# Hybrid mLSTM and latent-attention block on one core: nine changes to the order of splits, loads and turns beside an almost always busy TensorE

## The chip, the cores and the metric

One Trainium2 chip, one core of it. The metric is the device time of one execution in microseconds (us), as the median of several runs. A difference of 0.2% is 5.7 us here.

## The reference

One trunk layer of an encoder on 2048 tokens of width 1024, in f32:

```python
xn = rms_norm(h, ln_mix_g)
proj = xn @ w_in                           # 1024 -> 2512 columns
y_a = mlstm_group(q, k, v, o, gates, ...)  # 4 heads x 128, chunks of 128 tokens, both directions
y_b = mla_group(c_q, c_kv, k_rope, ...)    # latent attention, 4 heads, softmax over 2048 keys
h = h + concat([y_a, y_b]) @ w_out
h = h + (silu(gate) * val) @ w_down        # gate, val = dwconv3(rms_norm(h) @ w_up), width 2816
gate = sigmoid(rms_norm(h, ple_norm_g) @ w_ple_gate)
h = h + gate * rms_norm(p @ w_ple_proj, ple_post_g)
out = rms_norm(h, final_g)
```

## The kernel before

Every f32 product is made of three matmuls in a rounded f32 format: each operand is **split** into a high part (a cast on ScalarE, L121, or L129 with a factor) and a low part (source minus high part on VectorE, L124 or L130). Products of the big projections are made in **pairs** of output blocks by a seven-product scheme, whose operands are named A11, A12, A22, S1 to S4 (weights) and B11, B21, B22, T1 to T4 (activations); each pair runs a fixed sequence of products into the banks fx, fy, fz (L541 in the mLSTM projections, L1700 in output projection, MLP and gate). Between the products stand numbered calls `side(1)` to `side(7)`, which put other work into TensorE's order: transposes, splits, loads.

The stages, in order of time:

1. **in_proj**: 16 token tiles. For each, `rest` (product `bk<-wsr,xh`), `turn_rest` of the tile before (transposes `rtp`, L283), `vals` (product `bk<-wsp,xh`). POOL makes each tile's norm factor into a column of `rcol` (L142, L144). `norm_row` (L298) transposes 8 of these columns at once into a row, which is stored in `r_d` and read back as `rrow`. Beside it the activations' operands are made (`xsr`) and stored in `xo_d`.
2. **pairs** (twelve pairs): operands that don't stay resident are loaded from `xo_d` through four buffers `opr` and split in place; T3, T4 and B22 of the first half come through this queue during the first pair. `gates` is a generator whose steps (its yields) are run at every second side call; it makes the mLSTM gate factors and puts small matmuls (`fs<-ms`, L944) in between.
3. **queries**: for eight blocks c of 256 tokens, `latent` makes the no-rope queries (`qo`, L809), `rope` and `turn` the roped ones (`qro`, `qso`), stored in `q_d`. `attend_begin` starts attention inside this loop: it loads the first queries (`q_t`, L1145), splits them (`q_s`), and makes the first tile's scores (`bk<-kv,q_s`, L1163 to L1167).
4. **attend**: for every head and query tile the scores, maximum, exponential, transposes (`tb<-ident,pe`, L1227) and values (`ppv<-pt,kv`). The mLSTM runs beside it as a generator: at each of the order's pauses `pump` adds SIDE/(tiles x pauses) to an account, and one step of the generator runs when the account reaches one. SIDE is meant as the number of its steps. `pause(n)` yields n times. A chunk of the mLSTM loads `kn_d` into `kk` (w12), scales it (L999, in `state`), and at its end multiplies its sum `hh` by a factor, pauses, transposes it (`mb<-ident,hy`, L1130) and stores it.
5. **stream** (pairs -8 to 75): output projection (i < 0), up, down and gate. `up_prep` makes a pair's weight operands by `prep_a` and `prep_b`; `Out.turn` (L1998) transposes normalised tiles of the output projection, `Gate.turn` (L2122) tiles `ha` of the MLP's result into `gwr`.

TensorE's order is written out by hand (a manual schedule); what the other engines do follows the order in which the code issues it, with some instructions pinned to it (`keep_in_program_order`). All DMAs are issued from SyncE (SP). Buffers are fixed places: tags w, t, u, x with a number, each reused by many tiles, so that a place's new tile waits for the last reader of the one before.

## Time and profile before

| | us |
|---|---|
| median of 3 runs (lowest, highest) | 2856.83 (2855.85, 2857.14) |
| profiled execution | 2859.16 |
| its span | 2857.4 |
| outside the span | 1.76 |
| TensorE (PE) busy | 2816.5 (99%) |
| weight loads (PEld) busy | 2363.5 (83%) |
| VectorE (DVE) busy | 2131.6 (75%) |
| ScalarE (ACT) busy | 1581.6 (55%) |
| GpSimd (POOL) busy | 211.1 (7%) |
| DMA: mean rate, moved | 193 GB/s, 552.73 MB |

The profiled execution is 2.33 us above the median. A row of the timeline gives start, duration, engine, line, operation and `out<-in` by the program's names, how many equal instructions it stands for, and in brackets how long the engine was idle before it and what released it. A row of the table by windows gives each engine's busy time in a stretch, the granted TensorE clock (1.00 is full speed) and the busy share of the DMA engines.

### The profile page before, as it was taken

What the parts mean: (1) busy time and instruction counts of PE and PEld (TensorE: products, weight loads), DVE (VectorE), ACT (ScalarE), POOL (GpSimd) and SP (SyncE); (2) the same over time, 40 slices, a digit from 0 to 9 for tenths busy, and PEclk for the clock granted to TensorE, in tenths of its full rate; (3) what the DMA queues carried; (4) which work ended last, traced back from release to release, by engine and by line L of the source; (5) the groups of instructions that cost most, each with busy time, mean ns of one, the idle gap of its engine ahead of it and who ended that gap; (6) DMA issues with size and microseconds to landing.
All of it is one profiled execution on the core that took longest, in us unless ns stands there. A gap on an engine that the chain in (4) does not pass through costs nothing.

```text
span 2857.4 us, 39996 instructions
## 1 busy us (share of the span) xinstructions
PE 2816.5 (99%) x13932; PEld 2363.5 (83%) x13932; DVE 2131.6 (75%) x3702; ACT 1581.6 (55%) x3072; POOL 211.1 (7%) x331
## 2 busy tenths in 40 slices
PE   8999998999999999999999999999999999999998
PEld 7888887888888888888888888888888888888787
DVE  4877766777887777877778787777778767676787
ACT  6346765555566566655655556655556333254655
POOL 2100000000000000044200000000000000011012
PEclk9999999999999999999999999999999999999999
DMA  8883758554443333578735544667776757575864
GB/s 281 288 250 113 214 161 243 159 172 128 130 131 116 99 112 107 156 244 276 254 134 199 176 169 162 199 199 229 238 237 209 236 192 237 171 266 200 287 202 163
DMA packets 444531, 552.73 MB, mean 193 GB/s; under 512 B 34564, under 2 KB 296744, under 8 KB 444328
## 3 DMA queue, kind: packets, MB, share of 16 engines
q1 hardware_dynamic: 444328, 550.16, 60.1%
q8 instruction: 110, 1.80, 0.3%
q14 instruction: 93, 0.76, 0.1%
HBM read 357.45 MB, written 192.61 MB: 193 GB/s over the span
## 4 chain that ended last, share of the span: by engine, by line
PE 84%; DVE 4%; DMA 3%; ACT 2%; issue 1%; POOL 0%; SPq 0%; POOLq 0%; ACTq 0%; DVEq 0%
PE fy L1700 22%; PE fz L1700 15%; PE fx L1700 14%; PE ppv L1239 4%; PE tb L1227 3%; PE fy L541 3%; PE fz L541 2%; PE ppv L1240 2%; PE bk L1163 2%; PE bk L1165 2%; PE bk L1166 2%; PE bk L1164 2%; PE bk L1167 2%; PE fx L541 2%; PE fs L134 2%; PE mb L1101 1%
## 5 line engine op out<-in xcount | busy, mean ns | idle before, releaser
L1700 PE MATMUL fz<-op,fw 128*128 128x512 f32 x1968 | 479.3, 392 | 3.8 <-ACT fw L121 3.8
L1700 PE MATMUL fx<-op,fw 128*128 128x512 f32 x1968 | 476.0, 390 | 0.0
L1700 PE MATMUL fy<-op,fw 128*128 128x512 f32 x1968 | 475.2, 390 | 0.0
L1700 PEld LDWEIGHTS fz<-op,fw 128*128 128x128 f32 x1968 | 368.5, 188 | 81.9 <-ACT fw L121 5.0
L1700 PEld LDWEIGHTS fy<-op,fw 128*128 128x128 f32 x1968 | 368.7, 188 | 77.0 <-DVE fh L1685 0.5
L1700 PEld LDWEIGHTS fx<-op,fw 128*128 128x128 f32 x1968 | 368.4, 188 | 75.9
L121 ACT CAST pt<-tb 128x512 fp32r<-128x512 f32 x256 | 147.5, 586 | 187.9 <-PE tb L1227 187.0
L1700 PE MATMUL fy<-op,fwd 128*128 128x512 f32 (+1 forms) x984 | 238.1, 390 | 0.0
L1168 DVE TENSOR_REDUCE mx<-bk 128x1 f32<-128x512 f32 x256 | 175.4, 686 | 67.2 <-PE bk L1167 64.8
L1700 PEld LDWEIGHTS fy<-op,fwd 128*128 128x128 f32 x984 | 182.9, 188 | 37.7 <-DVE uv L1685 0.4
L124 DVE TENSOR_TENSOR pt<-tb,pt 128x512 fp32r<-128x512 f32 x256 | 173.5, 686 | 33.4 <-ACT pt L121 32.7
L1239 PE MATMUL ppv<-pt,kv 128*128 128x512 f32 x512 | 188.6, 407 | 1.0 <-DVE pt L124 1.0
L1185 ACT ACTIVATE pe<-bk,nm 128x512 f32<-128x512 f32 x256 | 174.7, 698 | 21.2 <-DVE nm L1179 21.1
L124 DVE TENSOR_TENSOR fw<-fwr,fw 128x1024 fp32r<-128x1024 f32 x124 | 150.9, 1221 | 34.0 <-ACT fw L121 32.7
L121 ACT CAST op<-opr 128x512 fp32r<-128x512 f32 x205 | 120.7, 620 | 81.2 <-DMA opr<-xo_d 16.6
L124 DVE TENSOR_TENSOR op<-opr,op 128x512 fp32r<-128x512 f32 x205 | 134.6, 690 | 25.7 <-ACT op L121 25.5
L1227 PE MATMUL tb<-ident,pe 128*128 128x128 f32 x1024 | 150.5, 273 | 1.5 <-DVE pt L124 1.3
L121 ACT CAST fw<-fwr 128x1024 fp32r<-128x1024 f32 x124 | 129.7, 1051 | 37.3 <-DVE fwr L1674 21.3
L1240 PE MATMUL ppv<-pt,kv 128*128 128x256 f32 x512 | 144.2, 282 | 0.0
L1227 PEld LDWEIGHTS tb<-ident,pe 128*128 128x128 f32 x1024 | 122.2, 141 | 20.4 <-DVE pt L124 4.1
L121 ACT CAST fw<-hraw 128x1024 fp32r<-128x1024 f32 (+1 forms) x72 | 70.2, 980 | 115.8 <-PE fx L1700 58.8
L1748 DVE SCALAR_TENSOR_TENSOR fgv<-uv,fcw,fgv 128x1024 f32<-128x1024 f32 x88 | 112.8, 1282 | 16.0 <-ACT fgv L1746 9.5
(407 smaller groups left out, 5210.1 us busy)
## 6 DMA issues: line engine op xcount, KB each, us to landing
fwr<-in_w_up SPq DMA_DIRECT2D x66, 512.0 KB
fh<-h_d SPq DMA_DIRECT2D x48, 512.0 KB
h_d<-fh SPq DMA_DIRECT2D x48, 512.0 KB
s_d<-fwr SPq DMA_DIRECT2D x44, 512.0 KB
fws<-s_d SPq DMA_DIRECT2D x44, 512.0 KB
rw<-row_d SPq DMA_DIRECT2D x32, 512.0 KB
tw_d<-tsum SPq DMA_DIRECT2D x60, 256.0 KB
opr<-tw_d SPq DMA_DIRECT2D x60, 256.0 KB
```

Source lines behind the costliest of these rows:

```text
L121: nc.scalar.copy(hi, src)
L124: (sub or nc.vector).tensor_tensor(lo, src, _f(hi), op=ALU.subtract)
L134: mm = lambda *a, **k: self.nc.tensor.matmul(*a, **k, skip_group_check=more)
L541: nc.tensor.matmul(out, a[:, k * P:(k + 1) * P], parts[lo], start=first, stop=lo == 1 and k == 3, skip_group_check=more)
L1163: mm(ps, ql, kh[:, ks], start=True, stop=False)
L1168: nc.vector.tensor_reduce(s.mx[:, kb:kb + 1], ps, axis=AX.X, op=ALU.max)
L1185: nc.scalar.activation(s.pe[:, kb % 2], s.banks[kb], AF.Exp, bias=s.nm, accum_out=s.rs[:, kb:kb + 1])
L1227: nc.tensor.transpose(t[:, j, :], s.p[kb][:, j * P:(j + 1) * P], self.ident)
L1239: mm(w.ps, vh[:, ks], pts[kb][:, j], start=kt == 0, stop=False, skip_group_check=True)
L1240: mm(w.ps[:, 0], vl[:, ks], pts[kb][:, j, 0], start=False, stop=kt == NT - 1, skip_group_check=True)
L1700: nc.tensor.matmul(out, a[:, k * P:(k + 1) * P], parts[lo][:, cols], start=first, stop=lo == 1 and k == last, skip_group_check=more)
L1748: nc.vector.scalar_tensor_tensor(t, u[:, tap:tap + 2 * SB], self.taps[:, tap, ct:ct + 1], t, op0=ALU.mult, op1=ALU.add)
```

## The change

Nine places, in order of time:

- **A** in_proj: `norm_row` of tiles 3 and 5 moves from ahead of the tile's first product to behind `turn_rest`.
- **B** T3 of the first half is loaded by four DMAs into places w12 and w13 at the start of the pairs, and split from there; the queue `opr` carries T4 and B22 only.
- **C** gates: one more yield ahead of the matmul `fs<-ms`.
- **D** queries: `attend_begin` is called one block earlier (c = 3). It loads there, splits at c = 4, and makes the scores at c = 5 as before. The queries' split lies in the second half of their own tile, not in w2 or u2. `split_c(7)` comes one block earlier, and the next scores stand behind all of block 7's products.
- **E** mLSTM in attention: `kk` alternates between w12 and w13; the ones column of the values is set once for each place, not for every chunk; one more pause ahead of the product with the factor; SIDE 695 for 678.
- **F** the late splits of output projection's operands are spread over its first pair's side calls; the scale of that pair's tiles is pinned in order.
- **G** Out's last transposes stand one side call later (4 and 5 for 3 and 4) from i = 1 on.
- **H** down's first pair: three steps of the next pair's preparation stand ahead of the load of T4.
- **I** gate's first pair: its transposes stand at sides 1 to 4 (before 1, 2, 4, 5), its weights' preparation behind side 4 (before 5), T2's load behind that; tile loads at 5 and 7, places w0 and w7 exchanged.

In-projection on PE, the difference at tile 3 (`wsr` and `wsp` are weights, `rtp` the transposes of `turn_rest`):

```order
 L134 MATMUL bk<-wsp,xh 128x512 x24
-L134 MATMUL bk<-wsr,xh 128x464
+L134 MATMUL bk<-wsr,xh 128x464 x24
+L283 MATMUL rtp<-ident,nn 128x128 x4
 L298 MATMUL tb<-ident,rcol 8x128
-L134 MATMUL bk<-wsr,xh 128x464 x23
-L283 MATMUL rtp<-ident,nn 128x128 x4
 L134 MATMUL bk<-wsp,xh 128x512 x24
```

The transpose of `rcol` stood behind one matmul of `wsr`, and stands behind all 24 and the four transposes now.

The DMA queue of SP in queries, before (`qso`, `qo` are stores of a block, `q_t` the loads of the first queries):

```order
L731 DMA qraw<-rest_d 128x2x256
L824 DMA q_d<-qso 64x2x256 x4
L811 DMA q_d<-qo 128x4x256
L731 DMA qraw<-rest_d 128x2x256
L824 DMA q_d<-qso 64x2x256 x4
L811 DMA q_d<-qo 128x4x256
L1145 DMA q_t<-q_d 128x512 x2
L824 DMA q_d<-qso 64x2x256 x4
```

and of the change:

```order
L736 DMA qraw<-rest_d 128x2x256
L829 DMA q_d<-qso 64x2x256 x4
L816 DMA q_d<-qo 128x4x256
L1154 DMA q_t<-q_d 128x512 x2
L736 DMA qraw<-rest_d 128x2x256
L829 DMA q_d<-qso 64x2x256 x4
L816 DMA q_d<-qo 128x4x256 x2
```

The two loads of `q_t` have moved ahead of one load of `qraw`, four stores of `qso` and one of `qo`.

PE at the start of the gate stage, before (tiles `ha` are transposed; `fwd` is the operand A22 of the pair before):

```order
L2122 MATMUL fs<-ident,ha 128x128 x4
L1700 MATMUL fy<-op,fwd 128x512 x9
L1700 MATMUL fy<-op,fw_24537 128x512 x3
L1700 MATMUL fy<-op,fw_24538 128x512 x3
L1700 MATMUL fy<-op,fw_24537 128x512 x3
L2122 MATMUL fs<-ident,ha 128x128 x4
L1700 MATMUL fx<-op,fw_24522 128x512 x3
```

and of the change:

```order
L2142 MATMUL fs<-ident,ha 128x128 x4
L1709 MATMUL fy<-op,fwd 128x512 x9
L2142 MATMUL fs<-ident,ha 128x128 x4
L1709 MATMUL fy<-op,fw_24445 128x512 x3
L1709 MATMUL fy<-op,fw_24446 128x512 x3
L1709 MATMUL fy<-op,fw_24445 128x512 x3
L2142 MATMUL fs<-ident,ha 128x128 x4
```

The third and the fourth group of transposes stand nine matmuls earlier each. The diff, without its unchanged lines:

```diff
@@ -35,7 +35,7 @@
...
 LAG_T, LAG_X, LAG_R = 1, 2, 2
-SIDE = 678
+SIDE = 695
 KSCALE = 128.0 ** -0.5
@@ -345,8 +345,6 @@
...
                 nc.vector.tensor_copy(self.cwt, pc)
-            if st in (3, 5):
-                norm_row(st // 2 - 1)
             if st == 7:
@@ -361,6 +359,8 @@
...
                 turn_rest(st - 1)
+            if st in (3, 5):
+                norm_row(st // 2 - 1)
             if st == NT - 2:
@@ -493,6 +493,9 @@
...
         self.PAIRS, self.npair = (("w3", "w4"), ("x11",), ("w5", "w6"), ("w8", "w9"), ("x10",)), -1
+        self.third = [self.at(t, [P, 2, SB], name="xt3") for t in ("w12", "w13")]
+        for k in range(4):
+            self.nc.sync.dma_start(self.third[k // 2][:, k % 2], self.xo_d[0, self.NAMES.index("T3"), k])
         self.pair_load(1)
@@ -593,7 +596,7 @@
...
-        begin(0, ("T3", "T4", "B22"))
+        begin(0, ("T4", "B22"))
         gates, prev = self.gates(), None
@@ -608,7 +611,9 @@
...
                 if i == 0 and at in (2, 3):
-                    load("T3", range(2))
+                    for k in (2 * at - 4, 2 * at - 3):
+                        self.xop["T3"][k] = self.in_place(0, "T3", k)
+                        self.split(self.third[at - 2][:, k % 2], *self.xop["T3"][k])
                 if i == 0 and at in (5, 6):
@@ -844,7 +849,7 @@
...
                     vv = self.split_latent(2, ("x10", "x11"), (c - 4,), None if c == 4 else vv)
-                if 0 < c < 7:
+                if 0 < c < 6:
                     split_c(c + 1)
@@ -852,11 +857,12 @@
...
                 latent(c, 1)
-                if c == 4:
+                if c == 3:
                     self.kr2, self.krl = kr
                     att = self.attend_begin()
-                    next(att)
-                if c > 4:
+                if c == 5:
+                    split_c(7)
+                if c > 2:
                     next(att, None)
@@ -939,6 +945,7 @@
...
         flip(o, b)
+        yield
         yield
@@ -982,11 +989,13 @@
...
+        values = [self.at(f"t{e}", [P, NH, 129], name="v1") for e in range(2)]
+        for v1 in values:
+            nc.vector.memset(v1[:, :, P:129], 1.0)
+
         def load_v(c):
-            v1 = self.at(f"t{c % 2}", [P, NH, 129], name="v1")
-            nc.sync.dma_start(v1[:, :, 0:P], self.v_d[c].rearrange("p (h e) -> p h e", h=NH))
-            nc.vector.memset(v1[:, :, P:129], 1.0)
-            return v1
+            nc.sync.dma_start(values[c % 2][:, :, 0:P], self.v_d[c].rearrange("p (h e) -> p h e", h=NH))
+            return values[c % 2]
@@ -1062,7 +1071,7 @@
...
             if c < NT - 1:
-                kk = self.at("w12", [P, 2, NH, P], name="kk")
+                kk = self.at(("w12", "w13")[c % 2], [P, 2, NH, P], name="kk")
                 if c == 0:
@@ -1121,7 +1130,7 @@
...
             r4 = self.rsq(ssq, NH, 1.0 / P)
-            yield from pause(2)
+            yield from pause(3)
             a = nc.vector.tensor_tensor(hh, hh, r4.unsqueeze(2).broadcast_to([P, NH, P]), op=ALU.mult)
@@ -1141,16 +1150,15 @@
...
         def load_q(h, pr):
-            q = self.at(f"w{4 - pr % 2}", [P, 2, 256], F32R, "q_t")
-            nc.sync.dma_start(_f(q), self.q_d[h, pr])
+            q = self.at(f"w{4 - pr % 2}", [P, 4, 256], F32R, "q_t")
+            nc.sync.dma_start(_f(q[:, 0:2]), self.q_d[h, pr])
             qv[h, pr] = q
...
             q = qv[h, pr]
-            qs = self.at("u2" if (h, pr) != (0, 0) else "w2", [P, 2, 256], F32R, "q_s")
-            self.split(_f(q[:, 0]), qs[:, 0], qs[:, 1])
-            qv[h, pr] = qs[:, 0], qs[:, 1], q[:, 1]
+            self.split(_f(q[:, 0]), q[:, 2], q[:, 3])
+            qv[h, pr] = q[:, 2], q[:, 3], q[:, 1]
@@ -1194,6 +1202,7 @@
...
         load_q(0, 1)
+        yield
         split_q(0, 0)
@@ -1795,6 +1804,9 @@
...
+                if i == blocks[0][0]:
+                    for _ in itertools.islice(self.late, 2):
+                        pass
                 bank = prev.spare if at % 2 and prev else s.spare
@@ -1811,9 +1823,6 @@
...
             nc.scalar.copy(s.y, x)
-            if i == blocks[0][0]:
-                for _ in self.late:
-                    pass
             if s.acc:
@@ -1832,6 +1841,10 @@
...
                 rest_z(prev)
+            ahead = self.prep_a(i + 1)
+            if i == NUP:
+                for _ in range(3):
+                    next(ahead)
             if j == 0 and blk:
@@ -1848,10 +1861,14 @@
...
                 next(steps[i])
-            load(then, "T2")
+            if i != NG - 1:
+                load(then, "T2")
             side(4)
-            if i + 1 < NG:
-                self.up_prep(i + 1)
+            if i + 1 <= NG:
+                for _ in chain(ahead, self.prep_b(i + 1)):
+                    pass
+            if i == NG - 1:
+                load(then, "T2")
             if 0 <= i < NG - 2:
@@ -1862,7 +1879,7 @@
...
             side(5)
-            if NG <= i + 1 < n:
+            if NG < i + 1 < n:
                 self.up_prep(i + 1)
@@ -1957,7 +1974,9 @@
...
         a = self.b.raw[i][e][:, 4:8].rearrange("p h t -> p (h t)")
-        self.nc.vector.tensor_tensor(a, a, self.rb[e], op=ALU.mult)
+        a = self.nc.vector.tensor_tensor(a, a, self.rb[e], op=ALU.mult)
+        if i == -8:
+            self.b.tc.keep_in_program_order(a)
@@ -2019,8 +2038,9 @@
...
             self.scaled(i - 1, int(at == 5))
-        if 0 < at < 5 and -8 <= i - 2 < 0:
-            self.turn(i - 2, *((1, 0), (1, 1), (0, 0), (0, 1))[at - 1], bank)
+        n = at - 1 if i < 1 or at < 3 else at - 2
+        if 0 <= n < 4 and -8 <= i - 2 < 0 and (at != 3 or i < 1):
+            self.turn(i - 2, *((1, 0), (1, 1), (0, 0), (0, 1))[n], bank)
         if -8 <= i - 2 < -4 and 3 < at < 7:
@@ -2100,7 +2120,7 @@
...
         b, nc = self.b, self.nc
-        h = self.ha[st] = b.at((self.places[2], "w1")[st] if st < 2 else ("w7", "w0")[st % 2], [P, D], name="ha")
+        h = self.ha[st] = b.at((self.places[2], "w1")[st] if st < 2 else ("w0", "w7")[st % 2], [P, D], name="ha")
         for f in range(2):
@@ -2268,16 +2288,18 @@
...
-        if -1 <= q < 7 and at in (1, 2, 4, 5):
-            e, f = divmod(at - 1 if at < 3 else at - 2, 2)
+        if -1 <= q < 7 and at in ((1, 2, 3, 4) if q < 0 else (1, 2, 4, 5)):
+            e, f = divmod(at - 1 if at < 3 or q < 0 else at - 2, 2)
             self.turn(i + 1, e, f, bank)
-            if f and q + e > -1 and 2 * q + e + 4 < NT:
+            if f and q > -1 and 2 * q + e + 4 < NT:
                 self.load_tile(2 * q + e + 4)
...
                          for f in range(2)]
+        if q == -1 and at == 5:
+            self.load_tile(2)
         if q == -1 and at == 7:
-            self.load_tile(2)
+            self.load_tile(3)
             self.load_pj()
```

## Prediction, on record before the changed kernel ran

> **What bounds the kernel now.** First the busy times of the page:
>
> ```profile
> PE 2816.5 (99%) x13932; PEld 2363.5 (83%) x13932; DVE 2131.6 (75%) x3702; ACT 1581.6 (55%) x3072; POOL 211.1 (7%) x331
> ```
>
> Then the table by windows: a window's length, busy time of PE, PEld, DVE, ACT and POOL, granted clock, DMA share and GB/s.
>
> ```profile
> 0.00:100.00 100.00, 91.66 (x420) 77.03 (x421) 56.86 (x138) 56.99 (x114) 20.38 (x52) 0.98 0.85 276
> 100.00:200.00 100.00, 100.00 (x474) 85.22 (x473) 77.71 (x182) 38.80 (x86) 12.43 (x18) 1.00 0.91 288
> ...
> 2260.00:2640.00 380.00, 380.00 (x1672) 313.84 (x1671) 257.39 (x384) 141.66 (x241) 21.70 (x48) 1.00 0.65 213
> ```
>
> TensorE sets the time: of the span of 2857.4 us it is idle for 40.9, and in the long stretches (2260 to 2640) for nothing, at 380 / 1672 = 0.227 us a matmul. The change removes no matmul. So all that it can give is idle time of PE, and time at a low clock. Next the waits of PE (total, times, longest):
>
> ```profile
> PE bk L1163 <- DVE q_s L124: 6.8, 1, 6.8
> PE tb L298 <- POOL rcol L144: 4.5, 2, 2.6
> PE fz L1700 <- ACT fw L121: 3.8, 3, 2.3
> PE mb L1130 <- DVE hy L1125: 2.2, 3, 1.0
> PE mb L1130 <- DVE v L988: 1.9, 1, 1.9
> PE fy L541 <- ACT ug L643: 1.6, 1, 1.6
> PE qpr L134 <- DVE nm L1179: 1.6, 1, 1.6
> ...
> PE fs L1998 <- POOL xt L1988: 1.2, 1, 1.2
> ...
> PE fs L944 <- DVE ms L939: 0.7, 1, 0.7
> ```
>
> These nine rows hold 24.3 us, at places that the change touches. Last the clock, in windows of PE alone (length, busy, clock, DMA share, GB/s):
>
> ```profile
> 46.10:49.50 3.40, 3.40 (x17) 1.00 1.03 340
> 71.46:74.88 3.42, 3.42 (x11) 0.50 1.00 381
> 206.10:209.50 3.40, 3.40 (x15) 1.00 0.33 80
> 470.20:474.20 4.00, 4.00 (x9) 0.50 0.92 282
> ...
> 699.52:702.93 3.41, 3.41 (x14) 0.50 0.53 87
> 2679.25:2682.66 3.41, 3.41 (x9) 0.50 0.83 272
> ```
>
> Behind four waits PE runs some 3.4 to 4 us at half clock though it is busy, and behind others it doesn't: a wait can cost more than its length.
>
> **The change, part by part.** The sum is made against the profiled execution (2859.16 us, of which 1.76 lies outside the span), then shifted to the median, 2.33 lower.
>
> **A, the transposes of rcol.**
>
> The timeline of PE at the first and at the second place:
>
> ```profile
> 46.07 0.27 PE L298 MATMUL tb<-ident,rcol 128*8 128x128 f32 x1 [2.59 <-POOL rcol L144]
> ```
>
> ```profile
> 70.38 0.27 PE L298 MATMUL tb<-ident,rcol 128*8 128x128 f32 x1 [1.96 <-POOL rcol L144]
> ```
>
> POOL is late with the last column, and PE's fixed order stands still for it. In the change 23 more matmuls of `wsr` and four transposes stand ahead. At 3.40 / 17 = 0.20 us (the window from 46.10) the 23 take 4.6 us, more than the 2.59 and 1.96 that were waited for, so both waits go. Behind the second came a half-clock window: 11 matmuls in 3.42 us where 11 x 0.20 = 2.2 would do, 1.2 lost. **Saves 2.59 + 1.96 + 1.2 = 5.8.** The store of the row and its reading back come some 5 us later; they lie beside 100 us of products. What is late next is DMA, share 0.85 to 0.91 (a rival below).
>
> **B, T3.** ACT's timeline, then PE's:
>
> ```profile
> 204.22 1.27 ACT L121 CAST op<-opr 128x512 fp32r<-128x512 f32 x2 [3.72 <-DMA opr<-xo_d]
> 205.41 0.58 ACT L643 COPY ug<-fy 128x512 f32<-128x512 f32 x1
> ```
>
> ```profile
> 206.04 3.01 PE L541 MATMUL fy<-op,fw 128*128 128x512 f32 x12 [1.58 <-ACT ug L643]
> ```
>
> ACT waits 3.72 us for a queued operand, and the copy that frees PE's bank stands behind those casts. With T3 in place the casts wait for nothing, and the copy is done before PE comes: **saves 1.6**. The four added loads are those that leave the queue, so bytes stay equal; but they are issued earlier, in a stretch with a DMA share of 0.91, ahead of weight loads. That is bounded at 0 and at the 1.6 itself; I take 0, since PE waits for nothing from 100 to 200.
>
> **C, gates.** The `fs<-ms` row gives 0.7, and its second matmul waited 0.2 behind it. 24 products (5.4 us) now stand ahead. **Saves 0.9.** Steps behind it move by one side call; the cover of products there is the same.
>
> **D, queries.** PE at the first scores, and at block 7's products:
>
> ```profile
> 461.77 1.60 PE L134 MATMUL bk<-cq,wq 128*128 128x256 f32 x12
> 470.20 0.80 PE L1163 MATMUL bk<-kv,q_s 128*128 128x512 f32 x1 [6.82 <-DVE q_s L124]
> ```
>
> ```profile
> 487.80 1.42 PE L134 MATMUL qpr<-wq,cq 128*128 128x256 f32 x10 [1.58 <-DVE nm L1179]
> ```
>
> PE has nothing from 463.4 to 470.2. Why, SP's and ACT's rows say: the first queries are loaded late.
>
> ```profile
> 465.40 1.54 SPq L1145 DMA_DIRECT2D q_t<-q_d  x2
> ```
>
> ```profile
> 469.28 0.40 ACT L121 CAST q_s<-q_t 128x256 fp32r<-128x256 f32 x1 [2.10 <-DMA q_t<-q_d]
> ```
>
> Issued at 465.4, the data is cast 3.9 later, the low part follows, and PE starts 0.9 after the cast began. In the new order of SP the load stands behind the store of the block before:
>
> ```profile
> 459.42 0.60 SPq L811 DMA_DIRECT2D q_d<-qo  x1
> ```
>
> So it is issued at about 460.0, cast at 463.9, and the scores start at 464.8 to 465.3 (ACT may be in a copy of 0.6 when the data lands). **A gap of 1.4 to 1.9 stays; I take 1.9**, nearer to the late end since DMA is at 0.92 there: 4.9 saved. The half-clock window (9 matmuls in 4.00 us, which at the 0.227 of 2260 to 2640 take 2.0) goes with it: 2.0. The wait of 1.58 at 487.8 goes, since the next scores no longer stand ahead of block 7's products. New is that these scores, the last transposes of `qro` and the exponentials crowd behind block 7: banks come free only when ACT and DVE have read them. No row shows this order; it is bounded by 0 and by two waits like that of 1.58, 3.2, and I take 1.6, one of them. **Saves 4.9 + 2.0 + 1.6 - 1.6 = 6.9**, with ends 8.5 and 3.3 (two new waits, and the half clock stays).
>
> **E, mLSTM in attention.** First DVE at the second chunk, then PE:
>
> ```profile
> 696.28 0.69 DVE L999 SCALAR_TENSOR_TENSOR kk<-kk,cols 128x512 f32<-128x512 f32 x1 [3.34 <-DMA kk<-kn_d]
> ```
>
> ```profile
> 698.30 0.66 PE L1130 MATMUL mb<-ident,hy 128*128 128x128 f32 x4 [1.89 <-DVE v L988]
> ```
>
> With one `kk`, its load had to wait until the chunk before had read it; DVE stood 3.34 us, then the factor's product (L1125) came late and PE waited 1.89. With two places the load starts a chunk earlier. The half clock behind it (14 matmuls in 3.41 us, some of them of 128 columns, so the full pace isn't in a row) cost between 0 and half, 1.7; I take 0.8. So 2.7. Of the `hy` waits (2.2 in three, longest 1.0) the added pause does the opposite of what it seems at first: it gives the squares' sum and POOL's root more of PE's work before DVE's queue stops at the product, but the transposes behind move with it, so the distance from product to transposes is the same three steps. What helps them are 30 memsets fewer on DVE and a DVE that is not stopped by an early wait; I take half, 1.1. The queries' split no longer waits for u2: 0, since no PE wait names it. The faster pace of side steps (695 / 678, 2.5%) only matches the added ones. **Saves 3.8**, with ends 0 and 5.8.
>
> **F, G, H.** The three `fz` waits are 2.3 in gate and 1.5 in two others (at the first pair of the output projection, F, and at down's first pair, H); G's wait is 1.2. In each the late work is put ahead of, or its use behind, a group of products of at least nine times 0.227, 2.0 us, more than the wait. **Saves 1.5 + 1.2 = 2.7**, with 0 as the other end where the late work is held up by its own input.
>
> **I, gate's first pair.** ACT, then PE:
>
> ```profile
> 2677.64 1.04 ACT L121 CAST fw<-gwr 128x1024 fp32r<-128x1024 f32 x1 [1.28 <-DVE gwr L1656]
> ```
>
> ```profile
> 2678.74 4.61 PE L1700 MATMUL fz<-op,fw 128*128 128x512 f32 x12 [2.34 <-ACT fw L121]
> ```
>
> The cast waits for DVE, and DVE for the turned tiles. The turns stand nine matmuls earlier, 2.0 us, and the chain behind them starts that much sooner; of the 2.34 some 0.3 stay, and I leave 0.8, since ACT has other casts of operands in between (ends 0 and 2.3). At 0.8 there is no half clock: 9 matmuls took 3.41 us there for 9 x 0.227 = 2.0, so 1.4. **Saves 1.5 + 1.4 = 2.9.**
>
> **Sum**: 5.8 + 1.6 + 0.9 + 6.9 + 3.8 + 2.7 + 2.9 = 24.6. The profiled execution goes from 2859.2 to 2834.6, the median from 2856.8 to **2832.2**.
>
> The windows also speak on a rule. PE at half clock follows idle of 1.89, 1.96 and 2.34 us, while 1.58 twice and even 2.59 were followed by full clock. The Trainium skill, TensorE: Matmul & The Clock Gate, section What's actually happening, lets the clock fall after at least one idle window of some 3.4 us, in a window that runs free of the kernel; idle below that would cost its length alone. The rows differ from the length it names, and with 2.59 they agree that the phase decides, not the length alone.
>
> **The rivals.**
>
> 1. *The half clock isn't tied to these short waits.* It would stay in some window of A, E and I, as phase or other load decide, and only idle time is won: 1.2 + 0.8 + 1.4 = 3.4 less, 2835.6. For it: 2.59 without a fall. Against: each of the four windows follows a wait, and the 1672 matmuls from 2260 to 2640 without one show clock 1.00. Chance 0.08. The page's rule would give this one.
> 2. *DMA takes the gain of A and B back.* If loads pace in_proj, PE that comes 5.8 earlier waits for its tiles instead: 24.6 - 7.4 = 17.2 saved, 2839.6. For it: share 0.91 from 100 to 200, 1.03 at 46.1. Against: PE waits for nothing there, and 9% of 100 us free is more than 5.8. Chance 0.14.
> 3. *Crowding in queries.* The first gap stays above 2 us and the half clock with it, or both new waits come: D at its lower end, 3.6 less, 2835.8. Chance 0.17.
> 4. *The mLSTM's end comes late at each chunk: slower.* One more pause and a denser side could put the transposes of `hy` ahead of DVE at every one of 16 chunks. At 1.89 and 0.8 of half clock each, as at 698.3, that is 43 us against 24.6 - 3.8 = 20.8: 2879. It decides from 20.8 / 16 = 1.3 us a chunk. The window of most chunks speaks for and against it:
>
> ```profile
> 720.00:1190.00 470.00, 466.10 (x2860) 403.50 (x2859) 367.19 (x894) 290.28 (x823) 37.12 (x52) 1.00 0.37 115
> ```
>
> DVE is the fullest engine beside PE (367 of 470), but PE is idle for 3.9 us in all there, and the product keeps its three steps to the transposes. Chance 0.05.
> 5. *Nothing to measure*: the waits reappear one product later everywhere (2857). The rows of order show the moved work; chance 0.03.
>
> **How the numbers follow.** My forecast, 2827 to 2837, has the remaining 0.53. A difference of 0.2%, 5.7 us, is about what a measurement can tell. Forecast and rivals 1 to 3 are faster by more (0.92); I lower that to 0.90 and put 0.05 on the same and 0.05 on slower, by rivals 4 and 5 and milder forms of both. Low end: D, E and I at their better ends (1.6 + 2.0 + 0.8) take off 4.4, and of the waits outside the nine rows (40.9 - 24.3 = 16.6 idle) some 5, which give 2823. High end: rivals 2 and 3 together, 2832.2 + 7.4 + 3.6 = 2843, and a quarter of a microsecond at each of 16 chunks, 2847.
>
> **What would show it.** PE's idle, 40.9 us, falls to about 21. The `rcol`, `ms`, `xt` and `ug` rows leave the waits; the first scores' wait reads 1.4 to 1.9, the gate's `fz` wait under 1; the row `kk<-kn_d` is gone on DVE at the first chunks. Clock is 1.00 from 100 to 2700. Wrong is the forecast if in_proj shows PE waits for `xh`, if the scores' wait is over 2 with a half-clock window behind it, if `mb<-ident,hy` waits come at most chunks, or if new names appear with more than 1 us.

## The result, and the profile after

| | before | changed |
|---|---|---|
| median, us (lowest to highest, 6 runs each) | 2855.96 (2853.23 to 2857.14) | 2845.33 (2843.98 to 2851.64) |
| profiled execution | 2859.16 | 2846.08 |
| its span | 2857.4 | 2844.3 |

The ratio is 0.9968, with a 95% interval of 0.9958 to 0.9979, which is 6 to 12 us. By the medians the changed kernel is 10.6 us faster, by the ratio 9, where 24.6 were forecast. The time lies in the stated range (2823 to 2847), at its slow end; the size was wrong by more than half.

The busy times of the changed kernel: of its span of 2844.3 us TensorE is idle for 33.5, where 21 were forecast.

```profile
PE 2810.8 (99%) x13932; PEld 2357.0 (83%) x13932; DVE 2133.1 (75%) x3673; ACT 1580.2 (56%) x3072; POOL 212.2 (7%) x331
```

The waits of PE in the changed kernel (total, times, longest):

```profile
PE mb L1139 <- DVE hy L1134: 3.2, 3, 1.6
PE tb L1236 <- DVE pt L124: 3.1, 5, 1.6
PE rtp L283 <- DVE nn L274: 2.0, 1, 2.0
PE fz L1709 <- DVE ug L1694: 1.8, 1, 1.8
PE bk L1171 <- DVE q_t L124: 1.6, 1, 1.6
PE fy L1709 <- DVE fh L1694: 1.5, 1, 1.5
PE fy L544 <- ACT fy L631: 1.3, 1, 1.3
```

The rows on `rcol`, `ms`, `xt` and `nm` are gone, as forecast, and the 6.8 us for the first queries are 1.6. But the waits for `hy` and `pt` in the mLSTM grew, and `rtp`, `fz`, `fy` have new names in the place of the old ones: the wait on `rcol` became one of `rtp` on `nn`, the wait on `fw` one on `ug` in down and one on `fh` in gate, the wait of `fy` on `ug` one on a copy. New names with more than 1 us are one of the signs of being wrong that the prediction gave.

The clock, in windows of PE alone (length, busy, clock, DMA share, GB/s), at two places that ran at 0.50 before:

```profile
71.46:74.88 3.42, 3.42 (x16) 1.00 1.00 388
461.60:465.00 3.40, 3.39 (x15) 1.00 0.93 288
```

No window of the changed kernel between its first and its last microseconds is below full clock. So the half clock went from this trace, as forecast; how much of it was there to be saved is a question for the first experiment. The waits didn't go as forecast.

Where the time went, by stage. The table gives the time from the start of one matmul to that of another, by their numbers in PE's order (0, 860, 2140, 2520, 6560, 7560, 11000, 11300, 13000, 13340 of 13932), as the mean over the traces in which that stage has the same code, with the lowest and highest and the number of traces (those of the experiments below are in it):

| stage (part) | before | changed | saved | forecast |
|---|---|---|---|---|
| in_proj (A) | 190.7 (189.0 to 191.7, 3) | 188.0 (186.6 to 191.3, 13) | 2.7 | 5.8 |
| pairs (B, C) | 267.1 (266.6 to 268.0, 5) | 267.5 (266.6 to 269.1, 13) | -0.4 | 2.5 |
| queries (D) | 71.2 (70.8 to 71.8, 4) | 63.4 (62.3 to 65.2, 14) | 7.8 | 6.9 |
| attention, D alone | 664.4 (663.7 to 665.4, 3) | 660.8 (660.6 to 661.1, 3) | 3.6 | 0 |
| attention, D and E | 664.4 | 664.5 (663.1 to 665.6, 6) | -0.1 | 3.8 |
| attention, E without D | 664.4 | 665.1 (1) | -0.7 | 3.8 |
| output projection (F, G) | 213.9 (213.2 to 214.2, 4) | 212.6 (212.0 to 213.3, 14) | 1.3 | 2.7 with H |
| down's start (H) | 71.0 (69.8 to 72.6, 6) | 71.2 (70.3 to 73.1, 10) | -0.2 | in the 2.7 |
| gate's start (I) | 76.1 (74.9 to 77.3, 4) | 74.6 (73.5 to 76.3, 12) | 1.5 | 2.9 |

The other stages are equal within 0.7 us. One stage with one code varies by 1 to 5 us from execution to execution, as much as most parts are worth.

### The profile page after: what moved, and what is told of

Read it like the earlier page. It is cut to its first block, busy times and chain, and to the rows that moved or that the text cites. A ratio compares the mean times of both kernels' runs of the same rounds, so it can differ in the third digit from the quotient of the medians.

```text
span 2844.3 us, 39914 instructions
## 1 busy us (share of the span) xinstructions
PE 2810.8 (99%) x13932; PEld 2357.0 (83%) x13932; DVE 2133.1 (75%) x3673; ACT 1580.2 (56%) x3072; POOL 212.2 (7%) x331
## 4 chain that ended last, share of the span: by engine, by line
PE 90%; DVE 4%; DMA 3%; issue 1%; ACT 1%; SPq 0%; POOL 0%; ACTq 0%; POOLq 0%; DVEq 0%
PE fy L1709 22%; PE fz L1709 15%; PE fx L1709 14%; PE bk L134 6%; PE ppv L1248 4%; PE tb L1236 3%; PE fy L544 3%; PE fx L544 2%; PE fz L544 2%; PE ppv L1249 2%; PE bk L1171 2%; PE bk L1173 2%; PE bk L1174 2%; PE bk L1172 2%; PE bk L1175 2%; PE fs L134 2%
## 5 line engine op out<-in xcount | busy, mean ns | idle before, releaser
L1709 PEld LDWEIGHTS fx<-op,fw 128*128 128x128 f32 x1968 | 368.1, 188 | 76.1
L1248 PE MATMUL ppv<-pt,kv 128*128 128x512 f32 x512 | 189.0, 407 | 1.0 <-DVE pt L124 1.0
```

What stands on the lines that cost most here:

```text
L1248: mm(w.ps, vh[:, ks], pts[kb][:, j], start=kt == 0, stop=False, skip_group_check=True)
L1709: nc.tensor.matmul(out, a[:, k * P:(k + 1) * P], parts[lo][:, cols], start=first, stop=lo == 1 and k == last, skip_group_check=more)
```

## The experiments

Each kernel was run beside the kernel before on one chip, but not all on the same chip, so ratios are compared and not times. Ratios are to the kernel before, with 95% intervals. Stage lengths and waits come from one trace of each kernel.

**The kernel before once more** (`before_again`), no edit.

> The kernel before once more, for a second trace. Theory (the first trace was a slow execution of it, so that part of the predicted saving was never there to be saved): TensorE idle time of this trace is 1 to 5 us under the 40.9 of the first, the waits for q_s, rcol, fw and hy are there again, but of other lengths. Rival (traces of one kernel agree): idle 40.9 within 0.5 and each of the nine waits within 0.2 us.

2854.06 us, ratio 0.9998 (0.9988 to 1.0008), span 2852.9, 4.5 less than the first trace; TensorE is idle for 39.1. Its waits:

```profile
PE bk L1163 <- DVE q_s L124: 6.8, 1, 6.8
PE tb L298 <- POOL rcol L144: 3.9, 2, 2.0
PE fz L1700 <- ACT fw L121: 3.2, 3, 1.6
...
PE mb L1130 <- DVE v L988: 1.6, 1, 1.6
```

and its clock:

```profile
45.96:49.37 3.41, 3.41 (x10) 0.50 0.98 364
71.46:74.88 3.42, 3.42 (x18) 1.00 1.03 385
465.80:472.62 6.82, 4.10 (x10) 0.50 0.96 301
699.52:702.93 3.41, 3.41 (x29) 1.00 0.83 276
2679.25:2682.66 3.41, 2.46 (x15) 1.00 0.86 329
```

The waits are the same ones, a little shorter, but the half clock stands behind the first `rcol` wait now (1.98 us), not behind the second (1.92), and behind neither of the two at 699 and 2679 (1.6 each). So the trace from which the forecast was made was a longer execution than this one: 2.2 us of its clock terms (0.8 in E, 1.4 in I) aren't there in another. The theory holds.

**D alone and D left out** (`d_alone`: the kernel before with D; `without_d`: the changed kernel with D undone).

```diff
-                if c == 4:
+                if c == 3:
                     self.kr2, self.krl = kr
                     att = self.attend_begin()
...
+                if c == 5:
+                    split_c(7)
+                if c > 2:
                     next(att, None)
...
-            qs = self.at("u2" if (h, pr) != (0, 0) else "w2", [P, 2, 256], F32R, "q_s")
-            self.split(_f(q[:, 0]), qs[:, 0], qs[:, 1])
+            self.split(_f(q[:, 0]), q[:, 2], q[:, 3])
```

> The kernel before with part D of the change alone (first queries loaded at block 3, second scores behind block 7). Theory (D is the one large term, and it is independent): the first scores' wait falls from 6.8 to 1.6 to 2.2 us, no half-clock window behind it, the wait of 1.6 on nm goes, two new waits at the second scores of 0.9 to 1.3 in all; 8 us less, about 2847. Rival (D only works with the other parts): under 4 us less, 2852.

> The changed kernel with part D undone, so the other eight parts alone. Theory (D alone brought the change its time, the eight others together bring nothing): 2852 to 2856, the same as before within 0.2%; the scores' wait of 6.8 us back. Rival (the eight others save at least a third of the 17.7 us forecast for them): 2849 or less.

`d_alone`: 2843.82 us, 0.9966 (0.9955 to 0.9978), 11.0 less than before: as fast as the whole change. `without_d`: 2852.99, 0.9991 (0.9981 to 1.0001), 1.8 less. So D is the change's gain, and the other eight parts, forecast at 17.7 us, sum up to nothing that these runs can tell from none. In the trace of D alone, the first scores and the second:

```profile
PE bk L1163 <- DVE q_t L124: 1.5, 1, 1.5
...
PE bk L1163 <- ACT pe L1185: 0.9, 1, 0.9
```

**A, and what takes half of it back** (`a_norm_row`: the kernel before with A; `no_sums`: the changed kernel without 16 subtractions of in_proj, those of the first half; `pool_sums`: the same subtractions, and those of the second half, on POOL). The three edits in that order:

```diff
-            if st in (3, 5):
-                norm_row(st // 2 - 1)
...
+            if st in (3, 5):
+                norm_row(st // 2 - 1)
```

```diff
-        tt, L, H = nc.vector.tensor_tensor, slice(0, SB), slice(SB, 2 * SB)
+        tt, L, H = lambda *a, **k: None, slice(0, SB), slice(SB, 2 * SB)
```

```diff
-        tt, L, H = nc.vector.tensor_tensor, slice(0, SB), slice(SB, 2 * SB)
+        tt, L, H = nc.gpsimd.tensor_tensor, slice(0, SB), slice(SB, 2 * SB)
```

> The kernel before, with part A of the change alone (the transposes of rcol behind 24 products). Theory (DVE's backlog gives half of A back): the two waits on rcol go, but the second rtp group behind them waits about 2 us for DVE's nn, as in the changed kernel; TensorE's lead over the kernel before is about 3.3 us at the end of in_proj, so about 2852.7 us. Rival (the terms of the prediction stand alone): 5.8 us less, 2850.2, and no wait of rtp over 0.5 us.

> The changed kernel with the 16 subtractions of in_proj for the first half's operands T1, T2, T3 and T4 left out, so those operands are not what the reference needs; nothing is put on another engine. Theory (DVE's queue makes nn late and gives back part of A): the rtp wait for DVE's nn, 1.4 to 3.0 us in the traces with this code, is under 0.5, and the lead at the end of in_proj grows by 1 to 2.5 us. Rival (the loads of x_t, or ACT's chain, make nn late): the rtp wait stays over 1.2.

> The changed kernel with in_proj's subtractions for the activations' operands on POOL, not on DVE. Theory (DVE's full queue in in_proj gives back half of A): the rtp wait for DVE's nn, 1.5 to 3.0 us in four traces with this code, falls under 0.5; lead at the end of in_proj grows by 1.5 to 2.5; about 2843.5. Rival (the loads of x_t set the pace there): the wait of rtp stays over 1.5 or moves to xh, 2845; slower if POOL's longer instructions end the chain to the stores later.

`a_norm_row`: 2854.04, 0.9994 (0.9984 to 1.0003). The trace has the new wait:

```profile
PE rtp L283 <- DVE nn L274: 1.8, 2, 1.2
```

It is in all 13 traces with A that leave DVE's work as it is, 1.3 to 3.6 us in all, and is at most 0.5 in the three without A. The row of DVE in the changed kernel shows how full its queue is there, 13.45 of 15.00 us:

```profile
70.00:85.00 15.00, 13.45 (x26) 1.00 0.79 278
```

`no_sums`: 2843.35, 0.9956 (0.9941 to 0.9971); the row on `nn` is gone, and in_proj takes 185.3 us, less than in any of the 13. So DVE's queue makes `nn` late, not the loads. How long in_proj would be without the subtractions and without A wasn't tried. `pool_sums` is no cure: 2862.24, 1.0027 (1.0016 to 1.0037).

```profile
PE rtp L283 <- DVE nn L269: 9.3, 2, 7.6
PE rtp L283 <- DVE nn L274: 2.4, 2, 2.0
```

In_proj takes 207.7 us with it. A subtraction takes 1.3 to 1.7 us on POOL (medians of its eight lines), where it takes 0.69 on DVE. POOL's own norm factors stand behind them, and DVE's waits for these (`nn` for `rsr`) are 11.4 us between 70 and 185, where they are 5.1 in the changed kernel. DVE's own instructions can grow too. Three times an `nn` of L276 that starts just behind a subtraction on POOL takes 1.34 to 1.36 us, as long as that runs; most take 0.35, though one of 1.44 stands beside none. One in the changed kernel, and one here, beside the subtraction that starts at 81.83:

```profile
77.85 0.35 DVE L276 SCALAR_TENSOR_TENSOR nn<-rs,rsr,gn 128x128 f32<-128x128 f32 x1 [0.87 <-POOL rsr L144]
```

```profile
81.90 1.34 DVE L276 SCALAR_TENSOR_TENSOR nn<-rs,rsr,gn 128x128 f32<-128x128 f32 x1 [2.25 <-POOL rsr L144]
```

**E in attention** (`kk_early`, `pause_back`, `early_and_pause`, `kk_back`, `pin_back`, `e_undone`, all from the changed kernel). By their times none of the six can be told from the changed kernel, since their intervals and its own overlap. The length of attention tells them apart: it is 663.1 to 665.6 us in the six traces with D and the whole of E. `kk_early` puts the load of the next chunk's `kk` into the middle of a chunk of the code:

```diff
+            if c + 1 < NT - 1:
+                nkk = self.at(("w12", "w13")[(c + 1) % 2], [P, 2, NH, P], name="kk")
+                nc.sync.dma_start(nkk[:, 0], self.kn_d[c + 1])
             cst = [cf, cb]
```

> The changed kernel, with the load of the next chunk's kk issued in the middle of the chunk before, where its second place is free. Theory (in the mLSTM DVE stands still at an instruction whose operand is still on its way, and the transposes of hy and the splits of pt behind it make TensorE wait): DVE's waits for kk from kn_d fall from 14.4 us to under 3, TensorE's waits for hy and pt from 6.3 to about 3.5, the time to about 2842.5. Rival (the added pause and SIDE set these waits): DVE's kk waits fall, TensorE's don't, 2845.

2843.93, 0.9961 (0.9948 to 0.9974); attention 661.6 us, not 664.5. DVE's wait for the loaded `kk`, in the changed kernel and here:

```profile
DVE kk L1008 <- DMA kk<-kn_d: 14.4, 9, 3.4
```

```profile
DVE kk L1008 <- DMA kk<-kn_d: 6.2, 8, 1.2
```

In the kernel before it was 7.6. It falls, but not under 3. PE's waits for `hy` and `pt` are 2.7; they are 6.3 in the changed kernel, and 3.7 to 6.3 in those six traces, of which its own is one. SP's rows show what the edit did: the load isn't issued half a chunk earlier against the work around it; it only stands ahead of the load of the values `v` and no longer behind it. The changed kernel, and `kk_early`, whose trace runs some 5 us ahead there:

```profile
978.99 0.52 SPq L997 DMA_DIRECT2D v<-v_d  x1
979.85 0.33 SPq L1078 DMA_DIRECT2D kk<-kn_d  x1
```

```profile
973.81 0.32 SPq L1101 DMA_DIRECT2D kk<-kn_d  x1
974.17 0.52 SPq L997 DMA_DIRECT2D v<-v_d  x1
```

`pause_back` takes back the pause and its pace:

```diff
-SIDE = 695
+SIDE = 678
...
-            yield from pause(3)
+            yield from pause(2)
```

> The changed kernel with pause(2) and SIDE 678 as before. Theory (DVE's stop at loaded operands is the cause): DVE's kk waits stay at 12 to 16 us and TensorE's waits for hy and pt between 5 and 8, 2844 to 2847. Rival (the added pause and the pace set them): TensorE's waits for hy and pt fall to the 3.5 us of before or less, 2842.

2843.78, 0.9959 (0.9946 to 0.9972); attention 661.7, `hy` and `pt` waits 3.7, DVE's `kk` waits 7.7. The time lies between the two forecasts. PE's waits are near the 3.5 of the rival, and DVE's fell as well, against the theory: this edit too shifts DVE's product against its load.

> The changed kernel with the early load of kk and with pause(2) and SIDE 678. Theory (both only take away DVE's stop at kk, so they don't add up): DVE's kk waits from kn_d under 7, TensorE's waits for hy and pt 2.5 to 4, the time that of either alone, 2843 to 2844. Rival (two causes that add): hy and pt waits under 1.5 and 2840 or less.

2843.17, 0.9953 (0.9938 to 0.9968); attention 661.6. The two don't add up, as the theory said, but DVE's `kk` waits are 10.5, not under 7, at `hy` and `pt` waits of 2.1. So the sum of DVE's stops over the stage isn't the measure: it is 7.6 in the kernel before and 7.7 with D alone, at 664.4 and 660.8 us of attention. What stands behind a stop decides, as the rows under D and E below show.

`kk_back` (w12 alone) and `pin_back` (no pinned scale):

```diff
-                kk = self.at(("w12", "w13")[c % 2], [P, 2, NH, P], name="kk")
+                kk = self.at("w12", [P, 2, NH, P], name="kk")
```

```diff
-        if i == -8:
-            self.b.tc.keep_in_program_order(a)
```

> The changed kernel with kk in w12 alone, the rest of E kept. Theory (the second place of kk moves DVE's product with kk ahead of its data and is what costs): attention 660 to 662, DVE's kk waits from kn_d 8 us or less. Rival (the added pause with SIDE 695 costs): attention stays at 664 to 666.

> The changed kernel without the pinned order of the first pair's scale. Theory (pinned, it makes DVE stand still for rb, 3.4 us, ahead of the product that the hy transposes at the end of the mLSTM wait for): the last hy wait of 1.6 us goes and attention is 1 to 2 us shorter, 662.5 to 663.5. Rival (unpinned it is put at a place as bad, as in the kernel before, 3.8 us of waits for rb): attention within 0.5 of 664.5.

`kk_back`: 2841.85, 0.9963 (0.9948 to 0.9977); attention 662.3.

```profile
DVE kk L1008 <- DMA kk<-kn_d: 8.0, 9, 1.3
```

With one place for `kk`, 2.2 of the 3.7 us between the whole change and D alone come back. With the second place kept, the old pause gives 2.8 (`pause_back`) and the early load 2.9 (`kk_early`). So the second place isn't the cause alone; it costs together with the pause and the place of its load. `pin_back`: 2846.82, 0.9974 (0.9964 to 0.9983), attention 663.9, and the last wait for `hy` stays, 1.4 where it was 1.6:

```profile
PE mb L1139 <- DVE hy L1134: 1.6, 2, 1.4
```

```profile
DVE yr L1977 <- DMA rb<-ri_d: 4.0, 2, 3.3
```

That theory falls: unpinned, the scale waits as long.

`e_undone` takes back `SIDE`, the pause, the second place of `kk` and the ones in front:

```diff
-        values = [self.at(f"t{e}", [P, NH, 129], name="v1") for e in range(2)]
-        for v1 in values:
-            nc.vector.memset(v1[:, :, P:129], 1.0)
...
+            nc.vector.memset(v1[:, :, P:129], 1.0)
```

> The changed kernel with part E undone whole (kk in w12, pause(2), SIDE 678, a memset for each chunk's ones). Theory (E costs in attention what D's tiles for the split queries save there): attention, 664.5 us on average in traces with E and 660.6 in the trace of D alone, is 660 to 662, the time 2841 to 2842.5. Rival (those 4 us are a matter of one execution): attention 664 or more, 2845.

2840.52, 0.9960 (0.9947 to 0.9973); attention 661.1. E as a whole cost what D had gained there. Without D it costs little: attention is 665.1 in `without_d` and 664.4 in the kernel before. So E takes back D's gain in attention, and has hardly a cost of its own.

**H and I** (`h_back`: the changed kernel without the steps ahead; `no_prep`: the changed kernel without the weights' sums and differences of the two pairs concerned; `pool_prep`: with these on POOL).

```diff
-            if i == NUP:
-                for _ in range(3):
-                    next(ahead)
```

```diff
+            if i in (self.NUP + 1, self.NUP + 24):
+                tt = lambda *a, **k: None
```

```diff
-        tt = nc.vector.tensor_tensor
+        tt = (nc.gpsimd if i in (self.NUP + 1, self.NUP + 24) else nc.vector).tensor_tensor
```

> The changed kernel without the three steps of preparation ahead of the load of T4 at down's first pair. Theory (DVE is full there, so order only decides which of its instructions is the last): the 1.8 us wait of fz for ug goes, a wait of 1.0 to 1.3 for the cast fw takes its place at the same product, and the time is 0.5 to 0.9 lower, about 2844.7. Rival (the steps ahead help as predicted): 1.1 slower, 2846.4.

> The changed kernel with the sums and differences for the weights S1 to S4 of the second down pair and the first gate pair left out (the output is not the reference's there). Theory (DVE is full at these two places, and the add that frees the bank stands behind this work): the waits of fz for ug (1.2 to 1.8) and of fy for fh (1.5) fall under 0.5 each; 2 to 3 us less than the changed kernel. Rival (the adds wait for TensorE or a load, not for DVE's queue): both waits stay over 1.0.

> The changed kernel with the weights' sums and differences of the second down pair and of the first gate pair on POOL. Theory (DVE is full at these two places, and its adds that free TensorE's banks come last): the waits of fz for ug (1.8) and of fy for fh (1.5) fall under 0.5 each; about 2842. Rival (the longer chain over POOL is last instead): waits of the same length for fw, 2845 to 2847.

`h_back`: 2844.87, 0.9958 (0.9942 to 0.9974), nothing that can be told from the change; the wait on `ug` is gone and waits of 0.9 on `fw` and 0.7 on `uv` stand there. `no_prep`: 2842.21, 0.9953 (0.9938 to 0.9968). Its waits in down and gate:

```profile
PE fz L1713 <- DVE ug L1698: 1.6, 1, 1.6
...
PE fz L1713 <- ACT fw L121: 1.3, 1, 1.3
...
PE fy L1713 <- DVE uv L1698: 1.3, 1, 1.3
...
PE fy L1713 <- DVE fh L1698: 0.5, 1, 0.5
```

The wait on `fh` (gate) falls from 1.5 to 0.5, that on `ug` (down) only from 1.8 to 1.6, and new ones come. So DVE's preparation isn't what sets down's wait, and the theory falls there. Gate's start is no shorter either, 74.7 us where the mean is 74.6. `pool_prep`: 2853.93, 0.9997 (0.9987 to 1.0006), with a new wait in down:

```profile
PE fy L1709 <- ACT c L1902: 4.4, 1, 4.4
```

What stands ahead of down's wait in both kernels is a stop of ACT for a loaded operand, here from 2190 to 2235 us, in the kernel before and in the changed one:

```profile
ACT op L121 <- DMA opr<-tw_d: 6.4, 4, 4.9
```

```profile
ACT op L121 <- DMA opr<-tw_d: 5.1, 1, 5.1
```

That this stop is the cause was read there and not tried.

**The parts that shorten their stage** (`adfgi`: A, D, the spread late splits, G and I; B, C, E, H and the pin undone).

> Only A, D, the spread late splits, G and I: the parts whose stages are shorter in the traces. From the stages' means over the traces: in_proj 3.1, queries 7.9, attention 3.8, output projection 1.2 and gate 1.2 less than before, 17.2 in all: 2837.6, faster than the changed kernel by 6 to 8. Rival (the parts hand their gain on to a wait in a later stage, as in_proj does in part): 2842 to 2845, like D alone.

2840.80, 0.9958 (0.9945 to 0.9971), 12.7 less than before on that chip by the medians; the changed kernel's ratio is 0.9968, and the two intervals overlap. As a saving that is the rival's result (10 to 13 less), not the 17.2 of the stages' means, though the time lies below the rival's 2842. In_proj (188.0), queries (62.8), attention (660.7), gate's start (74.0) are at or near their means; 2838.36 to 2844.30 is the spread of its runs. By the ratios it can't be told from `e_undone` (0.9960) or `early_and_pause` (0.9953).

## Why the forecast was wrong, by its steps

**The sum failed in the terms of A, B, C, H and I by one step that they share:** the products that now stand ahead last longer than the wait, so the wait goes. The named waits did go. But the comparison was between the products and the one wait, and not between the products and what came next, on the same engine or on another: that was late by a good part of the same time. E failed by another step, and D saved more than its term.

- **A** (5.8, measured 2.7 by the stage, 1.1 by the medians of A alone). The waits of 2.59 and 1.96 for POOL went, 1.3 to 3.6 came back at `rtp`, behind DVE's full queue: shown by `no_sums`. The two waits were also long in the first trace: 4.5 together, 3.9 and 3.4 in the two others without A. Rival 2 had it right that PE would come early and wait for its tiles, but what was late was DVE and not DMA.
- **B and C** (2.5, measured -0.4). `fy` waits for a copy behind other casts, 1.3, where it waited 1.6. That term was mis-sized as well: the wait is 0.6 to 0.9 in the four other traces without B, and 0.4 to 1.4 in those with it. At the gates a wait of 0.9 for `uv` takes the place of 0.7 for `ms`. Why wasn't tried.
- **D** (6.9, measured 7.8 in queries and 3.6 in attention). The mechanism was right and its rest of 1.6 lay between the 1.4 and 1.9 forecast, but the reason was another: the load is issued at 455.6, not at 460.0, and the cast stands behind ACT's `qo` copies. SP's, ACT's and PE's rows of the changed kernel:

```profile
455.59 2.27 SPq L1154 DMA_DIRECT2D q_t<-q_d  x2
```

```profile
460.12 0.59 ACT L814 ACTIVATE qo<-bk 128x512 f32<-128x512 f32 x1
460.60 0.71 ACT L121 CAST q_t<-q_t 128x256 fp32r<-128x256 f32 x2
```

```profile
461.61 0.47 PE L1171 MATMUL bk<-kv,q_t 128*128 128x512 f32 x1 [1.65 <-DVE q_t L124]
```

  The new waits at the second scores (0.9 and 0.3) were taken too high at 1.6. The 3.6 saved in attention were costed at nothing, "since no PE wait names it". The largest difference in the rows is at the second chunk, where the prediction had put the wait of 1.89 down to E. DVE stopped there for `kk` at 696.28, ahead of the product `hy` that PE's transposes need. DVE in the kernel before, and with D alone:

```profile
697.55 0.68 DVE L1125 TENSOR_TENSOR hy<-hy,rsr 128x512 f32<-128x512 f32 x1
```

```profile
679.61 0.69 DVE L1126 TENSOR_TENSOR hy<-hy,rsr 128x512 f32<-128x512 f32 x1
682.47 0.69 DVE L1000 SCALAR_TENSOR_TENSOR kk<-kk,cols 128x512 f32<-128x512 f32 x1 [2.17 <-DMA kk<-kn_d]
```

  With D the product `hy` stands ahead of the stop, in all three traces with D and without E; in all three without both it stands behind it, and PE waits 1.6 to 1.9. PE's idle time in attention is 6.6 to 7.0 us in the latter and 5.0 to 5.3 in the former, about half of the 3.6. What in D turned DVE's order, and where the rest comes from, stays open.
- **E** (3.8, measured -3.7 beside D, -0.7 without it). The step "with two places the load starts a chunk earlier" came true. Chunk 12's load (counted from 0) is issued at 979.85 in the changed kernel and at 1013.44 with one place (`kk_back`):

```profile
1013.44 0.32 SPq L1078 DMA_DIRECT2D kk<-kn_d  x1
1013.81 0.52 SPq L997 DMA_DIRECT2D v<-v_d  x1
```

  What failed is the step behind it, which the prediction didn't say: that DVE's product with `kk` stays where it was, so that its data is there. It moved a chunk earlier as well, right behind its load. Against what is said of the kernel above, DVE's order isn't that of the code here: chunk 12's product with `kk` (984.49) stands ahead of chunk 10's `hy` (986.96), though the code issues it two chunks later. DVE and PE of the changed kernel:

```profile
984.49 0.69 DVE L1008 SCALAR_TENSOR_TENSOR kk<-kk,cols 128x512 f32<-128x512 f32 x1 [3.36 <-DMA kk<-kn_d]
```

```profile
987.70 0.66 PE L1139 MATMUL mb<-ident,hy 128*128 128x128 f32 x4 [1.39 <-DVE hy L1134]
```

  So DVE still stops ahead of a `hy`, and longer: in the nine traces with two places and the load where the change has it in the code, SP issues at least 12 of the 14 loads of `kk` behind that of `v`, in the nine others all of them ahead of it. `kk_early`, `kk_back`, `pause_back` and `e_undone` each bring attention back to 661 to 662. It is the effect of rival 4 (late transposes of `hy`) in a mild form, by a stop for a load.
- **F, G and H** (2.7, measured 1.3 and -0.2): G's wait of 1.2 and F's went, H's was replaced; its cause is open. **I** (2.9, measured 1.5): the wait of 2.3 on `fw` became 0.5, and 1.5 of `fh` stand behind it, of which `no_prep` takes 1.0 without making the stage shorter.
- **The clock** (5.4 of the sum, in A, D, E and I): of this 2.2 was the luck of one trace. In the 18 traces the length of a wait doesn't tell whether a half-clock window follows: one follows idle of 1.96 in the first trace and not idle of 2.59 in the same one; one follows 1.60 in `adfgi` (at 2211.0) and none 2.49 in `pause_back` (at 83.7); one in `early_and_pause` begins at 1176.7, between two short waits of 1.14 and 0.74 (they end at 1174.9 and 1177.0). The Trainium skill, TensorE: Matmul & The Clock Gate, section What's actually happening, has a window that runs free of the kernel, and these traces agree with that; the rows here have the half clock behind single waits of 1.6 to 2.8, under the 3.4 us of idle that it names. The forecast said that the phase decides, and then used the phase of one execution as if it were the kernel's.

The shift to the median was also taken as a constant 2.33, though the first trace held waits and half clock that the second doesn't have.

## What to carry to other kernels

Where an engine that others wait for is nearly full, a wait that goes is worth only what the next late instruction leaves of it, on this engine or on another: look for the second latest before you book the first. A place more for a buffer lets its load start earlier, but brings something only if the instruction that reads it stays where it was; where that one moves ahead with the load, the engine stops for the load as before. And take two traces of the kernel before, because terms of one or two microseconds can belong to one execution.

## What the runs showed of the hardware

The half-clock windows come and go between executions of one program: 71.46 to 74.88 ran at 0.50 in one trace of the kernel before and at 1.00 in the other, behind waits of 1.96 and 1.92. The subtractions of in_proj that took 0.69 us each on DVE cost the kernel 17 us more on POOL by the two ratios (1.0027 and 0.9968), though POOL is busy for 7% of the span. Beside them three instructions `nn` of DVE took 1.34 to 1.36 us, where most take 0.35.
